# Gram matrices of the delta rule formed once for both directions, decay rows on all 128 partitions, constant buffer parts filled by GpSimd and ScalarE

## The chip, the core and the metric

One core of a Trainium2 chip (trn2). Its engines run their own instruction streams side by side: TensorE (PE; PEld is its weight load), VectorE (DVE), ScalarE (ACT), GpSimd (POOL) and SyncE (SP, which only issues DMAs here). The metric is the device time of one execution in microseconds, lower is better.

## The reference

One layer of a hybrid block over 2048 latent tokens of width 1024, with 256 context tokens ahead of them: a normalised and modulated input goes through one combined projection, then eight heads of softmax attention and four heads of a gated delta rule run in parallel on it, their outputs are normalised, concatenated and projected, and a gated feed-forward part follows. The change lies in the delta rule, which runs in both directions over the tokens:

```python
def chunk_gated_delta(q, k, v, g, beta, s0):
    """S_t = a_t (I - b_t k_t k_t^T) S_{t-1} + b_t k_t v_t^T, o_t = S_t^T q_t."""
    ...
    diff = g_cum[..., :, None] - g_cum[..., None, :]
    decay_incl = jnp.exp(jnp.where(incl, diff, -jnp.inf))
    decay_strict = jnp.where(strict, decay_incl, 0.0)
    k_beta = k * beta[..., None]
    lower = jnp.einsum("bhnid,bhnjd->bhnij", k_beta, k) * decay_strict
    t_inv = lax.linalg.triangular_solve(lower + eye, ..., left_side=True, lower=True, unit_diagonal=True)
    u = t_inv @ (v * beta[..., None])
    w = t_inv @ (k_beta * jnp.exp(g_cum)[..., None])
    ...
        intra = jnp.einsum("bhnid,bhnjd->bhnij", q, k) * decay_incl
    def step(state, xs_n):
        v_new = u_n - w_n @ state
        new_state = state * d_n + k_n^T @ v_new
        o_n = q_n @ state + a_n @ v_new

oc_f, s_ctx_f = chunk_gated_delta(qdc, kdc, vdc, gc_f, bec_f, s0)
oc_b, s_ctx_b = chunk_gated_delta(flip(qdc), flip(kdc), ..., s0)
ol_f, _ = chunk_gated_delta(qd, kd, vd, g_f, be_f, s_ctx_f)
ol_b, _ = chunk_gated_delta(flip(qd), flip(kd), ..., s_ctx_b)
o_gdn = gated_rms(ol_f + flip(ol_b), z_d, gdn_norm_g)
```

(The bodies are shortened; `step` is written here as matrix products.) The products `k k^T` and `q k^T` inside a chunk do not depend on the direction; the decays do.

## The kernel before

The program has three parts. Part one (to about 715 us of the trace) makes all projections and stores what the rest needs to DRAM: `qsc`, `ksc`, `vsc` for the attention, `gsc` (keys, queries and values of the delta rule in chunks of 128 tokens; `kd` is a piece on its way there) and `rsc` (decay rows). Part two (about 715 to 1780 us) is the attention and the delta rule together. Part three is output projection and feed-forward, to the end.

In part two `attention` takes 16 blocks of 128 queries. For each, `sm` products give a maximum (`mx`, `shift`), and then 18 pairs of key chunks follow: `sc` products (with `kh` and with `kx`, whose row 0 is a constant), the exponential `p`, its half-precision part `hp` and remainder `lp` (the latter a subtraction on GpSimd), and the products `ops` of `hp` and `lp` with the values `vst`. The number of a half and of its first key chunk stand in a name: `sc_15_1_6` is query block 15, second half, pair from chunk 6.

`delta(plan, d)` is one direction, d = 0 forward and d = 1 backward, in 18 steps of one chunk each: 2 of context, 16 latent. The two directions meet in the middle: step s of one and step 19 − s of the other work on the same latent chunk. A step loads `tT` (keys and queries, transposed), `tk` (keys and values scaled for this direction) and `rows`, 12 rows of decays, which the products `pdb`, `pdi` and `per` contract over 12 partitions to spread the decays over a 128x128 tile per head. `db` is the exponential of `pdb`; times the Gram matrix `pkk` it is the triangular matrix, which is split in `lh` and `ll` and inverted in steps (`m`, `t`, `pt`, `py`, `y`, `pa`, then `pr`, `r`, `pn`, `ti`). For latent chunks `at` is the exponential of `pdi` times the Gram matrix `pkq`. Then comes what depends on the state `s`: `pw`, `rv`, `pv`, `vn`, `pz`, the new `s`, and the output `po`, stored as `o` by the direction that comes first and added up as `fin` by the other. `y` are six buffers per direction that begin as unit matrices.

All instructions of part two are recorded (`Plan.add`; so their line in the trace is L403, where they are issued) and then issued in the order that a planner computes before the run (`Plan.order`): each engine takes, of the instructions whose inputs and ring buffers it thinks ready, the most urgent, with urgency from the track's weight. The tracks are `a` (attention, weight 1.0 by its share of work), `i0`, `i1` (what does not depend on the state, weight `IW`) and `d0`, `d1` (the rest, weight `DW`). `RINGS` says how many buffers a tile name has; the PSUM ring `g` of three banks serves all products of the delta rule, the ring `s` the `sc` products and `m` the `sm` products. On the chip each engine runs its stream in order and waits where an input is late. Loads of step 0 and the first attention loads are issued by GpSimd (`G`), all later ones by SP.

## Time and profile before

| | before |
|---|---|
| time, median of 3 runs (lowest, highest) | 3514.76 us (3511.21, 3516.85) |
| profiled execution: its time, its span in the trace | 3515.73 us, 3513.9 us |
| busy in the span: PE, DVE, ACT, POOL | 3355.6, 2298.6, 1639.6, 1410.7 us |
| mean granted clock of TensorE | 0.980 |
| part one, part two, part three (about) | 715, 1065, 1734 us |

The profile is of one execution. Busy times of PE are modelled at their ends, since matmuls are pipelined: the step from one start to the next is what an instruction advances the stream by. A row of waits is time that an engine stood idle, put down to what ended the wait.

### The profile page before, as it was taken

Reading aid. Unit: us, or ns where it says so; the run is one execution under the profiler, and the core shown is the slowest. Engines: PE = TensorE matmul, PEld = TensorE weight load, DVE = VectorE, ACT = ScalarE, POOL = GpSimd, SP = SyncE. Lnnn points to the kernel's source line nnn. Section 1 sums busy time; section 2 is a strip of 40 time slices with the busy share of each in tenths; the row PEclk is TensorE's granted clock in tenths of the full one; section 3 lists DMA queues with packets and bytes.
Section 4 is the critical chain, followed back from the end, with each engine's and each line's share of the span. In section 5 each row is a group of like instructions: output and inputs, shape, how many; then the busy total and the mean of one; then the engine's idle time right before and its main releaser. Section 6 shows DMA issues by size and latency. Waiting matters only on the chain.

```text
span 3513.9 us, 65298 instructions
## 1 busy us (share of the span) xinstructions
PE 3355.6 (95%) x26281; PEld 2715.5 (77%) x26281; DVE 2298.6 (65%) x3619; ACT 1639.6 (47%) x2556; POOL 1410.7 (40%) x1423
## 2 busy tenths in 40 slices
PE   6799999979999999999978999999999999999998
PEld 3799878857777777777756778888888888888898
DVE  5665577887777777777655567735773476447743
ACT  4443233447777676777644443323332333224331
POOL 4684455437767777777765411100110010001100
PEclk7899999989999999999989999999999999999999
DMA  6323335651111222220146643343334333433332
GB/s 227 90 66 97 120 116 149 189 153 48 60 63 55 66 63 70 66 65 29 53 145 218 218 159 96 95 130 112 120 97 124 115 116 97 125 114 120 96 108 91
DMA packets 209199, 381.30 MB, mean 109 GB/s; under 512 B 20360, under 2 KB 95720, under 8 KB 208624
## 3 DMA queue, kind: packets, MB, share of 16 engines
q1 hardware_dynamic: 207056, 371.74, 33.4%
q0 software_dynamic: 1840, 5.39, 0.6%
q8 instruction: 206, 3.38, 0.4%
q14 instruction: 97, 0.79, 0.1%
HBM read 297.73 MB, written 79.72 MB: 107 GB/s over the span
## 4 chain that ended last, share of the span: by engine, by line
PE 77%; DVE 8%; POOL 6%; DMA 4%; issue 3%; ACT 2%; SPq 0%; POOLq 0%; DVEq 0%; ACTq 0%
PE pu L520 9%; PE pu L519 9%; PE pu L521 9%; PE sc L403 6%; PE ops L403 5%; PE pdn L521 5%; PE pdn L520 5%; PE pdn L519 5%; PE po L403 3%; PE sm L403 3%; PE pa L403 1%; PE pg L520 1%; PE pg L519 1%; PE pg L521 1%; PE pkk L403 1%
## 5 line engine op out<-in xcount | busy, mean ns | idle before, releaser
L403 POOL TENSOR_TENSOR lp<-p,hp 128x1024 f16<-128x1024 f32 x288 | 616.0, 2146 | 232.8 <-DVE hp L403 88.0
L519 PE MATMUL pu<-h,ws_u 128*128 128x512 f32 x1408 | 550.5, 391 | 2.8 <-ACT h L403 2.8
L520 PE MATMUL pu<-h,ws_u 128*128 128x512 f32 x1408 | 549.0, 390 | 2.5 <-DVE h L403 2.5
L521 PE MATMUL pu<-h,ws_u 128*128 128x512 f32 x1408 | 548.5, 390 | 0.0
L403 DVE TENSOR_REDUCE mx<-sm 128x1 f32<-128x512 f32 x512 | 336.1, 681 | 74.7 <-PE sm L403 72.6
L1718 POOL COPY carry<-ue 128x2 f32<-128x2 f32 x132 | 24.8, 188 | 891.4 <-ACT ue L1716 891.4
L403 ACT ACTIVATE p<-sc 128x1024 f32<-128x1024 f32 x288 | 294.9, 1024 | 182.7 <-PE sc L403 173.3
L519 PEld LDWEIGHTS pu<-h,ws_u 128*128 128x128 f32 x1408 | 264.7, 188 | 60.1 <-ACT h L403 4.8
L520 PEld LDWEIGHTS pu<-h,ws_u 128*128 128x128 f32 x1408 | 264.6, 188 | 59.6 <-DVE h L403 4.2
L521 PE MATMUL pdn<-hid,ws_d 128*128 128x512 f32 (+2 forms) x880 | 307.4, 349 | 0.0
L520 PE MATMUL pdn<-hid,ws_d 128*128 128x512 f32 (+2 forms) x880 | 307.4, 349 | 0.0
L521 PEld LDWEIGHTS pu<-h,ws_u 128*128 128x128 f32 x1408 | 264.8, 188 | 54.9
L519 PE MATMUL pdn<-hid,ws_d 128*128 128x512 f32 (+2 forms) x880 | 306.4, 348 | 0.0
L1727 DVE SCALAR_TENSOR_TENSOR cv<-ue,cols,cv 128x512 f32<-128x512 f32 (+1 forms) x352 | 264.9, 752 | 15.8 <-DVE cv L1724 0.5
L1716 ACT COPY ue<-pu 128x512 f32<-128x512 f32 x176 | 103.2, 586 | 367.6 <-PE pu L521 367.0
L1690 DVE TENSOR_TENSOR ws_u<-raw_u,ws_u 128x1024 fp32r<-128x1024 f32 x176 | 214.5, 1219 | 19.1 <-ACT ws_u L1685 19.1
L403 PE MATMUL sc<-q,kh 128*128 128x512 f16 x576 | 218.7, 380 | 4.5 <-ACT p L403 3.9
L1724 DVE TENSOR_SCALAR cv<-ue,cols 128x512 f32<-128x512 f32 (+1 forms) x176 | 96.3, 547 | 188.3 <-ACT ue L1716 183.3
L403 PE MATMUL sc<-qx,kx 128*128 128x512 f16 x576 | 218.6, 380 | 0.0
L1715 POOL COPY ue<-carry 128x2 f32<-128x2 f32 x176 | 95.4, 543 | 291.6 <-DVE cv L1727 291.3
L1690 DVE TENSOR_TENSOR ws_d<-raw_d,ws_d 128x1024 fp32r<-128x1024 f32 (+1 forms) x96 | 109.0, 1136 | 157.8 <-ACT ws_d L1685 155.6
L403 ACT CAST hp<-p 128x1024 f16<-128x1024 f32 x192 | 200.8, 1047 | 3.3
(580 smaller groups left out, 8068.1 us busy)
## 6 DMA issues: line engine op xcount, KB each, us to landing
raw_u<-in_wu SPq DMA_DIRECT2D x176, 512.0 KB
raw_d<-in_wd SPq DMA_DIRECT2D x64, 512.0 KB
tk<-gsc SPq DMA_DIRECT2D x34, 512.0 KB
tT<-gsc SPq DMA_DIRECT2D x66, 256.0 KB
wm<-in_wm SPq DMA_DIRECT2D x64, 256.0 KB
gsc<-kd SPq DMA_DIRECT2D x64, 256.0 KB
raw_o<-in_wo SPq DMA_DIRECT2D x32, 512.0 KB
raw_d<-in_wd SPq DMA_DIRECT2D x32, 384.0 KB
```

Source lines behind the costliest of these rows:

```text
L403: fn(**{k: v.get() if isinstance(v, Lazy) else v for k, v in kw.items()})
L519: PE.matmul(out=ps, lhsT=hi_l(k), rhs=hi_r(k), start=st, stop=False)
L520: PE.matmul(out=ps, lhsT=hi_l(k), rhs=lo_r(k), start=False, stop=False)
L521: PE.matmul(out=ps, lhsT=lo_l(k), rhs=hi_r(k), start=False, stop=en)
L1690: V.tensor_tensor(out=made[u][:, 1, :n], in0=raws[u][:, :n], in1=made[u][:, 0, :n].bitcast(F32), op=ALU.subtract)
L1715: G.tensor_copy(out=ue[:, 0:2], in_=carry[:, b, :])
L1716: S.copy(out=ue[:, 2:514], in_=ps)
L1718: G.tensor_copy(out=carry[:, b, :], in_=ue[:, 512:514])
L1724: V.tensor_scalar(out=cv[:, :W], in0=ue[:, 0:W], scalar1=fw[0], scalar2=cols[:, C_FB + b:C_FB + b + 1], op0=ALU.mult, op1=ALU.add)
L1727: V.scalar_tensor_tensor(out=cv[:, :W], in0=ue[:, i:i + W], scalar=fw[i], in1=cv[:, :W], op0=ALU.mult, op1=ALU.add)
```

## The change

Three things change in part two, and two with them.

1. The direction that comes to a latent chunk first (`first`) copies each of its two Gram matrices from PSUM to a tile `gk` on ScalarE, and SP stores it to a new DRAM tensor `gmsc`. The other direction loads it (`gl`, two buffers) in place of its own products `pkk` and `pkq`.
2. The decay rows stand in two tiles of 128 partitions for the whole of part two, filled with zeros once; a step's load writes rows 0 to 11. The products contract over all 128 partitions.
3. The zeros of `rows`, `qx` and `kx` and the constant row of `kx` are filled by GpSimd ahead of its first loads, where VectorE filled `qx` and `kx` before. The `y` buffers are copied by ScalarE in place of VectorE.
4. `tk` has one buffer per direction in place of two.
5. `DW` and `IW` are 1.2 in place of 1.35, so the order of every engine in part two is another.

```diff
--- before.py
+++ after.py
@@ -36,12 +36,12 @@
 NJ = DFF // P
 EPS = 1e-6
 BIG = 1e30
-DW, IW = 1.35, 1.35
+DW, IW = 1.2, 1.2
 PSHIFT, PSLACK = 11.0, 6.5
 VTOP = 1024.0
 GTOP, ROWV, SC = 2048.0, 4096.0, 1024.0
 YB, UB = 3, 3
-RINGS = dict(s=1, m=2, o=1, g=3, p=4, hp=4, lp=4, q=2, h=4, fa=1, at=1, fb=2, tT=2, tk=2, st=2, t=2, ti=2, rw=1, fin=1)
+RINGS = dict(s=1, m=2, o=1, g=3, p=4, hp=4, lp=4, q=2, h=4, fa=1, at=1, fb=2, tT=2, tk=1, st=2, t=2, ti=2, fin=1)
 STAG = -0.03
 PATIENCE = dict(G=150.0, S=100.0)
 XB, LATER, KVW, DTB, PEC = 13, 3, 10.0, 5, 4.0
@@ -436,6 +436,7 @@
     ksc = dram.tile([NCK, P, KV, P], F16, name="ksc")
     vsc = dram.tile([NCK, P, 128], F32, name="vsc")
     zsc = dram.tile([NTT, P, 512], F32, name="zsc")
+    gmsc = dram.tile([NCK, 2, P, 512], F32, name="gmsc")
     osc = dram.tile([NTT, P, 512], F32, name="osc")
     osm = dram.tile([NTT, P, 512], F32, name="osm")
     oat = dram.tile([NTT, P, 512], F32, name="oat")
@@ -1070,11 +1071,11 @@
     pc = ExitStack()
     c2 = pc.enter_context(tc.tile_pool(name="c2", bufs=1, side="right", reuse_waits="tile"))
     kb = c2.tile([P, B_ER], BF16, name="kb")
-    er = c2.tile([12, P], BF16, name="er")
+    er = c2.tile([P, P], BF16, name="er")
     i16 = c2.tile([P, HG * P], F16, name="i16")
     lv16 = c2.tile([P, K_END - K_LV], F16, name="lv16")
     G.dma_start(out=kb, in_=kb_d[:, 0:B_ER])
-    G.dma_start(out=er, in_=kb_d[0:12, B_ER:B_END])
+    G.dma_start(out=er, in_=kb_d[:, B_ER:B_END])
     G.dma_start(out=lv16, in_=k32_d[:, K_LV:K_END])
     n16 = c2.tile([P, P], F16, name="n16")
     V.tensor_scalar(out=n16, in0=ident, scalar1=-1.0, scalar2=None, op0=ALU.mult)
@@ -1091,6 +1092,14 @@
     gf = p2.enter_context(tc.tile_pool(name="gf", bufs=5, reuse_waits="tile"))
     ap = p2.enter_context(tc.tile_pool(name="ap", bufs=4, side="right", reuse_waits="tile"))
     psa = p2.enter_context(tc.tile_pool(name="psa", bufs=1, space=PSUM, reuse_waits="tile"))
+    rows_t = [gs.tile([P, HG, 3, P], BF16, name=f"rows{d}", bufs=1) for d in range(2)]
+    qx_t = [ak.tile([P, HA, P], F16, name=f"qx{i}", bufs=1) for i in range(2)]
+    kx_t = ak.tile([P, NCK, KV, P], F16, name="kx", bufs=1)
+    for t in rows_t:
+        G.memset(t, 0.0)
+    for t in qx_t + [kx_t]:
+        G.memset(t[0:64], 0.0)
+    G.memset(kx_t[0:1], ROWV)
     plan = Plan(tc, psa)
     plan.patience, plan.rate, plan.fixed = PATIENCE, 2.34, (150, 55, 200, 170, 25)
 
@@ -1110,10 +1119,7 @@
             return plan.tile(psa, [P, 2, 512], F32, "s", n_, RINGS["s"])
 
 
-        qxs = [plan.tile(ak, [P, HA, P], F16, f"qx{i}", f"qx{i}", 1) for i in range(2)]
-        for t in qxs:
-            V.tensor_scalar(out=t[0:64], in0=ones[0:64, :].unsqueeze(1).broadcast_to([64, HA, P]), scalar1=0.0, scalar2=None,
-                            op0=ALU.mult)
+        qxs = [plan.wrap(t, [P, HA, P], F16) for t in qx_t]
 
         def load_q(qb):
             qt = plan.tile(aq, [P, HA, P], F16, "q", f"q_{qb}", RINGS["q"])
@@ -1126,16 +1132,12 @@
 
         q_now = load_q(0)
         kh = plan.tile(ak, [P, NCK, KV, P], F16, "kh", "kh", 1)
-        kx = plan.tile(ak, [P, NCK, KV, P], F16, "kx", "kx", 1)
+        kx = plan.wrap(kx_t, [P, NCK, KV, P], F16)
         for a in range(0, NCK, 6):
             src = ksc[a:a + 6].rearrange("c p f t -> p c f t")
             G.dma_start(out=kh[0:64, a:a + 6], in_=src[0:64])
             G.dma_start(out=kh[64:128, a:a + 6], in_=src[0:64])
         loaded.append(len(plan.ops) - 1)
-        for g in range(KV):
-            V.tensor_scalar(out=kx[0:64, :, g, :], in0=ones[0:64, :].unsqueeze(1).broadcast_to([64, NCK, P]), scalar1=0.0,
-                            scalar2=None, op0=ALU.mult)
-            V.tensor_scalar(out=kx[0:1, :, g, :], in0=ones[0:1, :].unsqueeze(1).broadcast_to([1, NCK, P]), scalar1=ROWV, scalar2=None, op0=ALU.mult)
         for a in range(0, NCK, 6):
             G.dma_start(out=kx[64:128, a:a + 6], in_=ksc[a:a + 6].rearrange("c p f t -> p c f t")[64:128])
 
@@ -1267,6 +1269,7 @@
     lv0 = lv16[:, 0:P].unsqueeze(1).broadcast_to([P, HG, P])
     bid = kb[:, B_ID:B_ID + P]
     o_l = [plan.wrap(osc[i], [P, 512], F32) for i in range(NTT)]
+    gm_l = [[plan.wrap(gmsc[i, j], [P, 512], F32) for j in range(2)] for i in range(NCK)]
 
     FT = {n: (t, RINGS[t]) for t, ns in (("fa", "db qe"), ("at", "at"), ("ti", "ti"), ("fb", "rv vn o")) for n in ns.split()}
 
@@ -1283,11 +1286,14 @@
         ys = [None]
         for l in range(1, 7):
             y = plan.tile(gh, [P, 512], F16, f"y{d}{l}", f"y{d}{l}", 1)
-            V.tensor_copy(out=y, in_=i16)
+            S.copy(out=y, in_=i16)
             ys.append(y)
         lvm = [None] + [lv16[:, P + 64 * (6 * d + l):P + 64 * (6 * d + l + 1)].bitcast(U16) for l in range(6)]
         ms = kb[:, (B_MSB if d else B_MSF):][:, :P].unsqueeze(1).broadcast_to([P, HG, P])
         mi = kb[:, (B_MIB if d else B_MIF):][:, :P].unsqueeze(1).broadcast_to([P, HG, P])
+
+
+        rws = plan.wrap(rows_t[d], [P, HG, 3, P], BF16)
 
         for step in range(NCK):
             ck = chunk_of(d, step)
@@ -1296,6 +1302,7 @@
             lat = ck >= NCC
             last = step == NCK - 1
             first = step < NCK + NCC - 1 - step if lat else step == 0
+            held = []
             q = SY if step else G
             plan.gate = None if step else loaded[0]
             tT = plan.tile(gin, [P, 2, 512], F32, f"tT{d}", f"tT_{nm}", RINGS["tT"])
@@ -1304,9 +1311,12 @@
                 SY.dma_start(out=tT[:, 1, :], in_=gsc[ck, :, 5, :])
             tk = plan.tile(gin, [P, 2, 512], F32, f"tk{d}", f"tk_{nm}", RINGS["tk"])
             q.dma_start(out=tk, in_=gsc[ck, :, 1 + 2 * d:3 + 2 * d, :])
-            rws = plan.tile(gs, [12, HG, 3, P], BF16, f"rows{d}", f"rows_{nm}", RINGS["rw"])
-            q.dma_start(out=rws, in_=rsc[d, ck].rearrange("h r s t -> r h (s t)"))
+            q.dma_start(out=rws[0:12], in_=rsc[d, ck].rearrange("h r s t -> r h (s t)"))
             plan.gate = None
+            if lat and not first:
+                for i in range(2):
+                    held.append(plan.tile(gin, [P, 512], F32, f"gl{d}", f"gl_{nm}_{i}", 2))
+                    SY.dma_start(out=held[i], in_=gm_l[ck][i])
 
             def bank(n_):
                 return plan.tile(psa, [P, 512], F32, "g", f"{n_}_{nm}", RINGS["g"])
@@ -1351,10 +1361,18 @@
             db = f32t("db")
             S.activation(out=db, in_=pd_, func=AF.Exp)
             def gram(i):
+
+                if held:
+                    return held[i]
                 pk = bank("pkq" if i else "pkk")
                 with plan.group():
                     for h in range(HG):
                         PE.matmul(out=pk[:, hs[h]], lhsT=tT[:, 0, hs[h]], rhs=tT[:, i, hs[h]], start=True, stop=True)
+                if not lat:
+                    return pk
+                gk = plan.tile(gin, [P, 512], F32, f"gk{d}", f"gk_{nm}_{i}", 1)
+                S.copy(out=gk, in_=pk)
+                SY.dma_start(out=gm_l[ck][i], in_=gk)
                 return pk
 
             V.scalar_tensor_tensor(out=db, in0=gram(0), scalar=-1.0, in1=db, op0=ALU.mult, op1=ALU.mult)
```

Three places show what stands where. TensorE at the start of step 12 of direction 0, a chunk that the other direction has had at its step 7: first before, where the four `rows` products are followed by the four products of the Gram matrix.

```order
L403 LDWEIGHTS kb_8056
L403 MATMUL pdb_0_12_19207<-kb_8056 128x512
L403 LDWEIGHTS rows_0_12_19146
L403 MATMUL pdb_0_12_19207<-rows_0_12_19146 128x128
...
L403 MATMUL pkk_0_12_19215<-tT_0_12_18593 128x128 x4
L403 MATMUL pv_0_11_19222<-rv_0_11_18610,ti_0_11_19203 128x128 x4
```

The same place now.

```order
L403 LDWEIGHTS kb_8057
L403 MATMUL pdb_0_12_19945<-kb_8057 128x512
L403 LDWEIGHTS rows0_8094
L403 MATMUL pdb_0_12_19945<-rows0_8094 128x128
...
L403 LDWEIGHTS t_1_11_19846
L403 MATMUL pa1_1_11_19954<-y11_8125,t_1_11_19846 128x64
```

The Gram product is gone; the weights come from the tile that stands for the whole part, and the stream goes on with the other direction's inversion.

GpSimd at the seam from part one to part two, with its DMA issues (`u` is the last piece of part one): before,

```order
L1055 MEMSET u_11_3_7999 128x1
L403 DMA q_0_8095<-qsc_61 128x1024
L403 DMA kh_8105<-ksc_62 64x6x256 x5
L403 DMA qx0_8129<-qsc_61 64x1024
L403 DMA kh_8105<-ksc_62 64x6x256
L403 DMA tT_0_0_8148<-gsc_60 128x512
L403 DMA rows_0_0_8150<-rsc_71 12x4x384
L403 DMA tT_1_0_8155<-gsc_60 128x512
L403 DMA rows_1_0_8158<-rsc_71 12x4x384
L403 DMA tk_0_0_8160<-gsc_60 128x1024
L403 DMA tk_1_0_8163<-gsc_60 128x1024
L403 DMA kx_8146<-ksc_62 64x6x256 x3
```

and now

```order
L1099 MEMSET rows0_8094 128x1536
L1099 MEMSET rows1_8095 128x1536
L1101 MEMSET qx0_8096 64x1024
L1101 MEMSET qx1_8097 64x1024
L1101 MEMSET kx_8098 64x4608
L403 DMA q_0_8107<-qsc_61 128x1024
L403 DMA qx0_8096<-qsc_61 64x1024
L403 DMA kh_8129<-ksc_62 64x6x256 x6
...
L403 DMA kx_8098<-ksc_62 64x6x256
L1102 MEMSET kx_8098 1x4608
L403 DMA kx_8098<-ksc_62 64x6x256 x2
L403 DMA tk_0_0_8186<-gsc_60 128x1024
```

Five fills stand ahead of the first load `q`, and the fill of the constant row stands between two loads of `kx`; the loads of `tk` have moved behind those of `kx`.

TensorE at the last product of the delta rule, `po` of step 17 of direction 1 (four of eight rows are left out): before,

```order
L403 LDWEIGHTS kx_8146
L403 MATMUL sc_15_1_6_27647<-qx1_8132,kx_8146 128x512
L403 MATMUL po_1_17_27654<-s_1_16_26590,tT_1_17_26592 128x128
L403 MATMUL po_1_17_27654<-vn_1_17_27610,at_1_17_27548 128x128
...
L403 LDWEIGHTS hp_15_1_4_27637
L403 MATMUL ops_15_1_27593<-vst_8624,hp_15_1_4_27637 128x65
```

and now

```order
L403 LDWEIGHTS q_15_26042
L403 MATMUL sm_15_1_0_2_27116<-kh_8129,q_15_26042 128x512
L403 MATMUL po_1_17_27118<-s_1_16_25534,tT_1_17_25478 128x128
L403 MATMUL po_1_17_27118<-vn_1_17_27038,at_1_17_26893 128x128
...
L403 LDWEIGHTS lp_14_1_14_27095
L403 MATMUL ops_14_1_26753<-vst_8551,lp_14_1_14_27095 128x65
```

Before, 20 `sc` products (five pairs of query block 15) stand behind it; now the `sc` products of all 18 pairs of block 15 do, 72 of them, with part of the block's `sm` products.

## Rows read from the trace of the kernel before

**Rows 1.** Busy time of the engines by stretch; columns: the stretch, its length, busy us of PE, PEld, DVE, ACT and POOL (with instructions), granted TensorE clock, busy share of the 16 DMA engines (1 is all, packets of two transfers can overlap), GB/s.

```profile
715.00:740.00 25.00, 10.46 (x46) 6.48 (x45) 17.55 (x33) 8.45 (x20) 5.37 (x7) 0.63 1.06 319
740.00:900.00 160.00, 152.04 (x2143) 114.09 (x2142) 134.98 (x243) 109.53 (x152) 99.19 (x54) 0.97 0.16 50
900.00:1740.00 840.00, 829.54 (x11797) 624.02 (x11796) 636.25 (x1131) 600.92 (x774) 611.14 (x322) 1.00 0.20 61
1758.00:1780.20 22.20, 12.67 (x181) 8.15 (x178) 7.75 (x8) 11.13 (x15) 19.88 (x14) 0.84 0.20 49
```

**Rows 2.** Waits of PE from 757 to 1758 us, the largest entry: us in total, times, longest.

```profile
PE pt L403 <- DVE t L403: 5.1, 8, 1.4
```

**Rows 3.** Gram products. First the timeline of PE from 763 us (start, us, then the instruction, xcount), then PE's groups by shape from 720 to 1785 us (xcount | busy us, mean ns | idle before).

```profile
763.21 1.16 PE L403 MATMUL pkk<-tT 128*128 128x128 f32 x8
764.21 0.38 PE L403 MATMUL sm<-kh,q 128*128 128x512 f16 x1
764.42 0.38 PE L403 MATMUL sc<-q,kh 128*128 128x512 f16 x1
...
L403 PE MATMUL pkk<-tT 128*128 128x128 f32 x288 | 41.6, 289 | 2.6 <-DVE s L403 1.4 <-ACT db L403 1.2
...
L403 PE MATMUL pkq<-tT 128*128 128x128 f32 x256 | 35.3, 281 | 0.0
```

**Rows 4.** Timeline of PE around the decay rows, 1748.5 to 1752 us.

```profile
1749.20 0.38 PE L403 MATMUL pdi<-kb 128*128 128x512 bf16 x1
1749.51 0.39 PE L403 MATMUL pdi<-rows 12*128 12x128 bf16 x4
1749.83 1.16 PE L403 MATMUL pkq<-tT 128*128 128x128 f32 x8
...
1751.25 0.40 PE L403 MATMUL pn<-r,t 128*128 128x128 f16 x4
1751.48 0.41 PE L403 MATMUL ops<-vst,lp 128*128 128x65 f16 x8
```

**Rows 5.** Weight loads of the decay rows, by shape, 720 to 1785 us (xcount | busy us, mean ns | idle before, what ended it).

```profile
L403 PEld LDWEIGHTS <-rows 12*128 12x128 bf16 x272 | 15.1, 93 | 23.8 <-issue 23.0 <-DMA vraw<-vsc 0.8
...
L403 PEld LDWEIGHTS <-er 12*128 12x128 bf16 x128 | 7.1, 92 | 9.6 <-issue 9.1
```

**Rows 6.** The seam: timeline of PE, of DVE and of POOL (idle before it and what ended that in brackets), the fill that is nearest to the new ones (min/median/max ns), and the issue row of `kh` from 703 to 740 us (queue, xcount, KB each, median us from issue to landing).

```profile
710.69 0.60 PE L958 MATMUL pt<-k,y 128*128 128x128 f32 x4
...
720.14 1.12 PE L958 MATMUL pt<-k,y 128*128 128x128 f32 x4 [4.28 <-ACT y L1022]
729.33 1.11 PE L958 MATMUL pt<-k,y 128*128 128x128 f32 x4 [8.07 <-ACT y L1022]
730.24 1.06 PE L403 MATMUL sm<-kh,q 128*128 128x512 f16 x2
...
719.55 2.01 DVE L403 TENSOR_SCALAR qx<-k 64x1024 f16<-64x1024 f32 x2
721.49 2.60 DVE L403 TENSOR_SCALAR kx<-k 64x2304 f16<-64x2304 f32 x2
...
706.16 0.54 POOL L403 DMA_DIRECT2D q<-qsc  x1 [0.36 <-issue]
706.70 3.30 POOL L403 DMA_DIRECT2D kh<-ksc  x5
...
L897 POOL MEMSET rt<- x2: 3934/3934/3935, 306.2 to 326.7; 72x4608 bf16 x2
...
kh<-ksc POOLq DMA_DIRECT2D x6, 192.0 KB, 5.6
```

**Rows 7.** The chain of work that ended last, pieces from 717 to 738 us (start, us, what).

```profile
718.07 16.69 DMA gsc<-kd
...
737.31 0.61 ACT db L403
```

**Rows 8.** VectorE from 740 to 1758 us: an operation with one input in PSUM, and two with both in SBUF; xcount: duration ns min/median/max, first and last start.

```profile
L403 DVE SCALAR_TENSOR_TENSOR db<-pkk,db x35: 659/681/692, 739.5 to 1724.5; 128x512 f32<-128x512 f32 x35
...
L403 DVE TENSOR_TENSOR m<-lh,lv x36: 411/1024/2160, 740.1 to 1727.1; 128x512 f16<-128x512 f16 x36
...
L403 DVE TENSOR_TENSOR t<-i,m x36: 407/776/1750, 741.3 to 1728.0; 128x512 f16<-128x512 f16 x36
```

**Rows 9.** Timeline of all engines at 1796 us (part three), POOL and DVE.

```profile
1796.29 2.34 POOL L403 TENSOR_TENSOR ws_o<-raw_o,ws_o 128x1024 fp32r<-128x1024 f32 x1
1796.35 2.82 DVE L403 SCALAR_TENSOR_TENSOR oraw<-oraw,oss,rows 128x512 f32<-128x512 f32 x1 [1.06 <-POOL oss L403]
```

**Rows 10.** ScalarE's copy of a 128x512 product out of PSUM, by shape, 740 to 1740 us (xcount | busy us, mean ns | idle before).

```profile
L403 ACT COPY vn<-pv 128x512 f32<-128x512 f32 x35 | 20.4, 583 | 13.0 <-PE pv L403 12.5
```

**Rows 11.** One `tk` load: timeline of PE, SP and DVE from 1520 to 1530 us, and the busy tenths of the DMA engines in 40 slices of 1521.9 to 1529.9 us.

```profile
1521.09 1.06 PE L403 MATMUL pz<-vn,tk 128*128 128x128 f32 x8
...
1522.18 0.32 SPq L403 DMA_DIRECT2D tk<-gsc  x1
...
1529.06 1.13 DVE L403 SCALAR_TENSOR_TENSOR rv<-pw,kbe,tk 128x128 f32<-128x128 f32 x4
...
DMA  0000009913599976100000000000000000957899
```

**Rows 12.** Timeline of POOL at the end of the attention.

```profile
1773.02 6.73 POOL L403 TENSOR_TENSOR lp<-p,hp 128x1024 f16<-128x1024 f32 x3
```

## Prediction, made before the changed kernel was run

> **What bounds the kernel now.** I read the windows first, to find the stage that the change touches. From 740 to 1740 us, where both directions of the delta rule run beside the attention, TensorE (PE) is busy 829.54 of 840 us and 152.04 of 160, at a granted clock of 1.00 (the upper of its two levels, 2.4 GHz) and 0.97; VectorE, ScalarE and GpSimd are near three quarters, and the DMA engines at a fifth [rows 1]. The waits of PE come next: over 1,001 us the largest entry is 5.1 us, behind the delta chain's `t` [rows 2]. So PE's own instruction stream is the limit there, and work taken off it is time, as long as no other engine comes up to it. Two stretches are of another kind: the seam before the stage, 715 to 740, with PE busy 10.46 of 25 us and the DMA engines full, and its end, 1758 to 1780, with five attention pairs left, GpSimd busy 19.88 of 22.2 us and PE 12.67 [rows 1].
>
> **The change, part by part.**
>
> *Grams.* Each latent chunk's two Gram matrices are now formed by the direction that comes first; 32 of 68 groups leave PE (eight records each: 36 groups of `pkk`, 32 of `pkq`). From the start of one `pkk` to the next instruction is 764.21 − 763.21 = 1.00 us; the engine's busy time gives 41.6/36 = 1.16 and 35.3/32 = 1.10, modelled ends included [rows 3]. A 512-column half-precision product beside it advances 0.21, so nothing else hides in the 1.00. That piece enters from a 12-row group, which the next term counts, so I take 0.93: 32 × 0.93 = **−30 us** (bounds −28 and −32).
>
> *Decay rows on 128 partitions.* The columns streamed do not change, only the height of the array in use. Going into the 12-row group, a 512-column product advances 1749.51 − 1749.20 = 0.31 instead of 0.21; coming out, four products advance 1749.83 − 1749.51 = 0.32, where four of the same width at full height (`pn`) advance 1751.48 − 1751.25 = 0.23 [rows 4]. So a group of short rows costs 0.10 + 0.09 = 0.19 us beyond its work. The weight loads say the same from the other side: 272 loads of `rows` stand idle 23.8 us and 128 of `er` 9.6, nearly all put down to issue [rows 5]. There are (272 + 128)/4 = 100 groups, hence 100 × 0.19 = **−19 us**; if the gap is the group's own and not its height's, 0.
>
> *The seam.* VectorE loses the fills of `qx` (2.01 us) and `kx` (2.60 for the zeros alone) and twelve copies, which stood between the last pieces of the projections: PE waited 4.28 and 8.07 us for `y` there, and its first attention product came only at 730.24. GpSimd gets five fills ahead of `q`. The nearest row, a fill of 72x4608 bf16, takes 3.93 us [rows 6]; by columns that makes 1.31 twice for `rows`, 0.87 twice for `qx`, 3.93 for `kx`, 8.3 us, and another 3.93 between two loads of `kx`. By the order the first fill waits for the last projection tile but one, whose products end where `pt` begins, at 710.69; so `q` is issued near 719 instead of 706.16, and the last `kh`, 4 to 5 us behind it, near 724. The `kh` loads took 5.6 us to land [rows 6], so `sm` starts near 730 as before. What ends the seam is not that but the store of `kd`, 16.69 us in the chain, with the last `kd` and a table load between its end and `db` at 737.31 [rows 7]; the store ran while the DMA engines were full [rows 1]. With VectorE's queue 5 us shorter and the loads of `kx`, `tk` and `vraw` later than the stores, the last `kd` is done some 5 us sooner. I take **−4 us** (bounds −8, and +13 if the loads behind the fills decide).
>
> *The held Grams on VectorE.* The 32 `db` and `at` operations of the second direction now read two SBUF tiles; with PSUM they take 681 ns with hardly any spread [rows 8]. The two-SBUF-input product `m` has 411 least, 1024 in the middle and 2160 at most [rows 8]. One pair of rows shows how: GpSimd starts `ws_o` at 1796.29 for 2.34 us, VectorE's `oraw` with two SBUF inputs starts 0.06 later and lasts 2.82, 0.5 past GpSimd's end [rows 9]. The Trainium skill, page "SBUF — State Buffer", section "Who interferes with whom", states it as a rule: a VectorE instruction with two SBUF inputs contends with a GpSimd instruction that reads SBUF, and the later issuer is blocked for the whole of the other. Here the trace agrees, and the rule speaks against this part of the change.
> On average I add what `m` has over its least, 0.6 us, plus 0.1: 32 × 0.7 = 22 us more on VectorE, in its second 500 us. What reaches PE is far less: `m` and `t` together already lose about 36 × (0.6 + 0.4) = 36 us so, and PE waits 5.1 us for `t` [rows 2, 8]. That ratio gives 22 × 5/36 = 3; I take **+4** (bounds 0 and 68, the latter 32 × (2.82 − 0.68), rows 8 and 9 at their worst).
>
> *Copies on ScalarE.* 32 copies of a Gram at 583 ns, the time of `vn` from PSUM [rows 10], are 19 us in the first half, on an engine that is 72% busy; twelve `y` copies are some 7 us at the seam, where it is busy 8.45 of 25 [rows 1]. A Gram's PSUM bank is held a copy longer. **+3** (0 to +10).
>
> *Stores and loads.* 64 transfers of 256 KB are 17 MB in a stage whose DMA share is 0.20 [rows 1]: no cost in bandwidth. Two new waits: SP's queue holds each store until its copy is done, with the prefetches behind it, which are issued well ahead of their use; and step 10 of one direction needs step 9 of the other through DRAM. **+1** (0 to +4).
>
> *One `tk` buffer.* The load can now be issued only after `pz`. In the trace the issue stands at 1522.18, just behind `pz` (1521.09, 1.06 long), and the next reader `rv` at 1529.06; its transfer shows as busy slices of 0.2 us from the seventh to the eighteenth after 1521.9, so it is in by 1525.5 [rows 11]: 3.3 us from the issue, of 6.9. In the new order `pw` stands 1 to 5 us of PE work behind `pz` in the first ten steps, so some ten loads are late by a fraction. **+3** (0 to +10).
>
> *The order.* The lower weights let the attention take turns earlier; before, the last delta product stood ahead of the last five pairs, now ahead of eighteen. There PE has no delta work to fill the wait for `lp`, and GpSimd needs 6.73/3 = 2.24 us a pair [rows 12] and the same 19.88 − 11.2 = 8.7 us of output work: 18 × 2.24 + 8.7 = 49 us. PE's part is at most 18 × 12.67/5 = 46 and, at the upper clock instead of 0.84, some 38. So PE waits 3 to 11 us there, against 22.2 − 12.67 = 9.5 now [rows 1]. **+1** (−6 to +8).
>
> *Sum:* −30 − 19 − 4 + 4 + 3 + 1 + 3 + 1 = −41. The profiled execution took 3515.7 us, 1 us above the median of the runs; 3515.7 − 41 = **3475 us**, 1.2% less. Nothing after 1785 us is touched.
>
> **Rivals.**
> - *The held Grams lock VectorE against GpSimd (slower).* The place is steps 10 to 17 of both directions, the price up to 2.14 us each. Without that term the sum is −45; it turns the sign when 45/32 = 1.4 us of each reaches PE, and at 2.14 the time is 3515.7 − 45 + 68 = 3539. For it: GpSimd is busy 73% of the stage and one `lp` lasts 2.1 us. Against it: the 7-to-1 cushion above, and an average delay near 0.7. 6 in 100. The rule of the Trainium skill's page "SBUF — State Buffer" named above would give this case if each operation met a fresh `lp`.
> - *The bare tail drags.* If eighteen pairs run like the last five (22.2/5 = 4.4 us each), the tail is 80 us instead of 49: 3475 + 31 = 3506, still faster. For it: nothing but attention is there to cover a wait. Against it: two thirds of the pairs lie ahead of the output work that slowed those five. 10 in 100.
> - *The rows change does nothing,* because the 0.19 us belong to loading new weights in small groups: 3494. Against it, `pn`, also four small products, has no such gap. 8 in 100.
> - *The seam waits for GpSimd's fills:* +13 instead of −4, 3492. 10 in 100.
> - *The work leaves PE, but the stage does not shorten,* since the reordered chains of the two directions now meet their latencies: PE has stalled little, yet a step's chain of some 25 dependent links fills its slot. Giving back all 49 us means 3515 to 3525, no change or a little slower. 7 in 100.
>
> **How the numbers follow.** The forecast has 59 in 100 and its own range, with about half of the terms at their nearer bounds at once, 3462 to 3488. The whole range takes in the rows, seam and tail cases and leaves out the two bad ones: 3456 to 3506. About 0.2%, 7 us, is what a measurement of this kernel can tell from no change. Faster by more than that: the forecast and the three mild cases, 87 in 100. Within it: half of the last case and a few near the turning point of the first, 5. Slower: 8.
>
> **What would show it.** Right: `pkk` and `pkq` with 544 − 32 × 8 = 288 records together; the `rows` loads with their issue idle near nothing; PE's busy time of the stage down by about 45 to 50 us and its waits much as before; first `db` earlier than 737.3; `db` and `at` in a second, longer form from the held tiles. Wrong: PE waits for `db`, `at` or `t` of tens of us in the second half (the lock); waits for `lp` above 20 us at the end (the tail); a wait of PE on `tk` or `gl` loads. The prediction fails most easily where I had no row: the latencies of the new order.

## The result, and the profile after

The changed kernel takes 3489.72 us (median of 6 runs, 3483.83 to 3492.77) against 3517.35 us of the kernel before beside it: a ratio of 0.992 [0.9905, 0.9934], 28 us less. A second set of runs gave 0.9927 [0.9915, 0.9939]. The forecast was 41 us less, 3475 us, within 3456 to 3506.

Parts one and three, which the change hardly touches, differ by several us from one execution to the next (part three lasted from 1731 to 1743 us in the profiled executions), so I compare part two inside each trace: from the start of the last projection product `pg` to that of the first `pto` product of part three. That is 1065.2 us before, and 1037.1 us after (1040.3 in the second profile): 25 to 28 us, the whole difference.

The windows of the kernel before, cut at the first `pdb`, half-way to the last `po`, at the last `po` and at the first `pto` (stretch, length, busy us of PE first):

```profile
715.00:732.20 17.20, 4.32 (x17) 2.47 (x16) 14.87 (x28) 4.32 (x12) 4.74 (x6) 0.59 1.05 299
732.20:1245.00 512.80, 498.44 (x7036) 376.76 (x7035) 396.77 (x715) 362.27 (x490) 344.11 (x184) 0.99 0.20 64
1245.00:1757.50 512.50, 505.45 (x7175) 377.70 (x7172) 384.06 (x676) 365.82 (x461) 381.05 (x199) 1.00 0.18 57
1757.50:1780.20 22.70, 13.17 (x191) 8.64 (x190) 8.25 (x8) 11.13 (x15) 19.99 (x16) 0.84 0.19 48
```

and of the changed kernel, cut at the same places of the program:

```profile
711.60:726.40 14.80, 4.99 (x21) 2.87 (x20) 8.66 (x13) 12.43 (x29) 14.21 (x15) 0.77 1.01 274
726.40:1211.00 484.60, 467.64 (x6787) 361.23 (x6786) 375.90 (x684) 364.01 (x492) 340.24 (x185) 0.99 0.25 80
1211.00:1694.80 483.80, 465.36 (x6792) 353.16 (x6790) 408.68 (x677) 354.50 (x464) 368.91 (x192) 0.99 0.28 87
1694.80:1748.70 53.90, 39.55 (x561) 24.14 (x559) 26.06 (x32) 33.49 (x37) 47.27 (x28) 0.96 0.11 26
```

PE's busy time in part two fell from 1021.4 to 977.5 us, so 44 us of work left it; its idle time (length less busy) rose from 43.8 to 59.6. The second profile of the changed kernel (e5 below) has 980.2 and 60.1, 41 us less work. By stretch, the idle time went from 12.9 to 9.8 us at the seam, 14.4 to 17.0 in the first half, 7.1 to **18.4** in the second half, 9.5 to **14.4** at the end. VectorE does more in the second half than it did in the longer one before: 408.68 of 483.8 us against 384.06 of 512.5.

The work that left, in PE's groups by shape and the weight loads (answers [rows 3, 5]; xcount | busy, mean ns | idle before):

```profile
L403 PE MATMUL pkk<-tT 128*128 128x128 f32 x160 | 21.9, 280 | 0.0
...
L403 PE MATMUL pkq<-tT 128*128 128x128 f32 x128 | 17.3, 278 | 0.0
...
L403 PEld LDWEIGHTS <-rows 128*128 128x128 bf16 x272 | 20.8, 98 | 10.3 <-issue 0.6 <-DMA rows<-rsc 0.4
...
L403 PEld LDWEIGHTS <-er 128*128 128x128 bf16 x128 | 9.2, 98 | 1.4 <-issue 0.5
```

288 Gram records are left of 544. The idle put down to issue ahead of the `rows` and `er` loads went from 32 us to 1, all idle ahead of them from 33.4 to 11.7. The first `db` exponential, a sign that the prediction named, comes at 727.0 us in place of 737.3. A piece of PE's timeline shows both prices (answers [rows 3, 4]):

```profile
728.19 0.38 PE L403 MATMUL pdb<-kb 128*128 128x512 bf16 x1
728.40 0.39 PE L403 MATMUL pdb<-rows 128*128 128x128 bf16 x4
728.63 1.11 PE L403 MATMUL pkk<-tT 128*128 128x128 f32 x8
729.57 0.78 PE L403 MATMUL sm<-kh,q 128*128 128x512 f16 x2
```

The 512-column product ahead of the rows now advances 0.21 us in place of 0.31, the four rows products 0.23 in place of 0.32, and a Gram takes 0.94.

The products with a loaded Gram on VectorE (answers [rows 8]; min/median/max ns). From 1240 to 1690 us their means are 1.30 us for `db` and 1.72 for `at`:

```profile
L403 DVE SCALAR_TENSOR_TENSOR db<-gl,db x16: 679/1236/2283, 1233.9 to 1636.7; 128x512 f32<-128x512 f32 x16
...
L403 DVE TENSOR_TENSOR at<-gl,at x16: 676/1912/2652, 1279.1 to 1681.3; 128x512 f32<-128x512 f32 x16
```

One place shows how such a product comes to hold up TensorE (timelines of POOL, DVE and PE):

```profile
1329.13 2.14 POOL L403 TENSOR_TENSOR lp<-p,hp 128x1024 f16<-128x1024 f32 x1 [0.28 <-POOL lp L403]
1329.53 2.28 DVE L403 SCALAR_TENSOR_TENSOR db<-gl,db 128x512 f32<-128x512 f32 x1 [0.18 <-ACT db L403]
...
1334.02 2.27 POOL L403 TENSOR_TENSOR lp<-p,hp 128x1024 f16<-128x1024 f32 x1
1334.57 2.01 DVE L403 TENSOR_TENSOR t<-i,m 128x512 f16<-128x512 f16 x1
1336.63 0.40 PE L403 MATMUL pt<-i,t 128*128 128x128 f16 x4 [1.51 <-DVE t L403]
```

The held `db` starts 0.4 us behind an `lp` of GpSimd and ends 0.54 us past its end; `t`, which also reads two SBUF tiles, does the same 5 us later. VectorE has no pause between the two, and PE waits 1.51 us for `t`. Of the 17.3 us of waits that PE's list has in the second half, 16.2 end with a VectorE instruction. I followed VectorE's work without a pause back from each of these, up to 12 us: what the held products there take beyond 0.68 us covers 12.3 of the 16.2 us, counting no wait for more than its length. That is a bound from above, since other work stands in the same stretches.

### The profile page after: what moved, and what is told of

It is laid out like the page before. It is cut to its first block, busy times and chain, and to the rows that moved or that the text cites. A ratio compares the mean times of both kernels' runs of the same rounds, so it can differ in the third digit from the quotient of the medians.

```text
span 3482.1 us, 64968 instructions
## 1 busy us (share of the span) xinstructions
PE 3309.7 (95%) x26025; PEld 2692.3 (77%) x26025; DVE 2312.2 (66%) x3601; ACT 1661.9 (48%) x2600; POOL 1432.9 (41%) x1429
## 4 chain that ended last, share of the span: by engine, by line
PE 73%; DVE 10%; POOL 6%; DMA 4%; issue 3%; ACT 3%; SPq 0%; POOLq 0%; DVEq 0%; ACTq 0%
PE pu L521 9%; PE pu L522 9%; PE pu L520 9%; PE sc L403 6%; PE ops L403 5%; PE pdn L522 5%; PE pdn L521 5%; PE pdn L520 5%; PE po L403 3%; PE sm L403 2%; PE pa L403 1%; DVE mx L403 1%; PE pg L522 1%; PE pg L521 1%; PE pg L520 1%
## 5 line engine op out<-in xcount | busy, mean ns | idle before, releaser
L403 POOL TENSOR_TENSOR lp<-p,hp 128x1024 f16<-128x1024 f32 x288 | 623.3, 2172 | 212.2 <-DVE hp L403 66.9
```

What stands on the lines that cost most here:

```text
L403: fn(**{k: v.get() if isinstance(v, Lazy) else v for k, v in kw.items()})
```

## The experiments

Every kernel below is the changed one but for the lines shown, except e3 and e6, which start from the kernel before. Part two is measured as above; idle is PE's, for the seam, the two halves and the end.

| kernel | ratio to before, 95% interval | part two, us | idle: seam, first, second half, end |
|---|---|---|---|
| before | 1 | 1065.2 | 12.9, 14.4, 7.1, 9.5 |
| changed | 0.9920 [0.9905, 0.9934] | 1037.1 | 9.8, 17.0, 18.4, 14.4 |
| e5 the same again | 0.9927 [0.9915, 0.9939] | 1040.3 | 10.3, 17.2, 18.5, 14.2 |
| e1 exponentials in PSUM | 0.9904 [0.9892, 0.9917] | 1030.3 | 10.4, 16.5, 12.0, 12.6 |
| e2 six `lp` on VectorE | 0.9937 [0.9925, 0.9949] | 1037.3 | 10.8, 16.5, 18.3, 12.7 |
| e3 rows alone | 0.9974 [0.9966, 0.9983] | 1054.3 | 12.6, 16.9, 8.0, 12.6 |
| e4 weights 1.35 | 0.9936 [0.9923, 0.9949] | 1040.5 | 10.2, 15.9, 17.8, 14.0 |
| e6 Grams alone | 0.9965 [0.9952, 0.9977] | 1050.3 | 13.1, 11.9, 13.7, 11.6 |
| e7 weights 0.85 | 0.9919 [0.9905, 0.9932] | 1035.7 | 11.1, 16.5, 19.2, 9.2 |
| e8 fills and copies back | 0.9917 [0.9903, 0.9930] | 1037.4 | 12.6, 18.0, 13.1, 13.3 |
| e9 `y` copies on VectorE | 0.9933 [0.9920, 0.9945] | 1037.3 | 10.5, 16.2, 18.4, 13.2 |
| e10 e1 and e9 | 0.9894 [0.9879, 0.9909] | 1029.7 | 10.5, 16.2, 12.1, 12.9 |
| e11 e10, weights 0.85 | 0.9878 [0.9864, 0.9892] | 1023.3 | 12.1, 15.6, 7.6, 10.3 |
| e12 e10, output work on VectorE | 0.9898 [0.9884, 0.9912] | 1028.9 | 10.0, 16.3, 12.1, 12.9 |

**e1: the ports.** Where a Gram is loaded, the exponentials stay in PSUM:

```diff
-            S.activation(out=db, in_=pd_, func=AF.Exp)
+            S.activation(out=pd_ if lat and not first else db, in_=pd_, func=AF.Exp)
-            V.scalar_tensor_tensor(out=db, in0=gram(0), scalar=-1.0, in1=db, ...)
+            V.scalar_tensor_tensor(out=db, in0=gram(0), scalar=-1.0, in1=pd_ if held else db, ...)
```

(and the same for `at` with `pd2`; the lines are shortened).

> The changed kernel, with one difference: where a Gram matrix is loaded, the exponentials db and at are left in their PSUM bank, so that VectorE's product reads one SBUF tile and one PSUM bank. No instruction is added or removed; the bank is held until the product is done. Theory A (the two-SBUF products wait for GpSimd, and that reaches PE): the held db and at fall from means of 1.30 and 1.72 us to about 0.68, VectorE gets back 26 us, PE's waits between 1240 and 1680 us fall from 16 us towards the 4 us of the kernel before, and the time falls by 8 to 15 us against the changed kernel (ratio to before about 0.988 to 0.990 in place of 0.992). Theory B (the waits come from the new order and the meeting of the two directions, not from the ports): db and at get shorter all the same, but PE's waits stay at 12 us or more and the time within 4 us.

The products lost their spread (min/median/max ns), and the second half of the mixed stretch its idle time in part:

```profile
L403 DVE SCALAR_TENSOR_TENSOR db<-gl,pdb x16: 667/678/689, 1237.5 to 1629.1; 128x512 f32<-128x512 f32 x16
...
L403 DVE TENSOR_TENSOR at<-gl,pdi x16: 670/677/689, 1283.3 to 1673.6; 128x512 f32<-128x512 f32 x16
...
1204.00:1681.10 477.10, 465.10 (x6848) 354.01 (x6845) 390.77 (x688) 357.51 (x467) 361.90 (x192) 1.00 0.28 88
```

Idle there is 12.0 us in place of 18.4, part two 7 to 10 us shorter, the ratio 0.002 lower. By the time that is theory A, at or just under the low end of its 8 to 15 us; the waits went about half of the way that it gave them. One doubt remains: the longer hold of the bank also changes the planner's order (TensorE's stream is another from about the middle on, with 21 pairs behind the last `po`), and e8, with another order and the old products, has 13.1 us there too. So how much of the 6.4 us is the ports and how much the order was not separated. Over all kernels the sign of the edit holds: with the old products part two lasts 1035.7 to 1040.5 us in four orders (e4, e7 and e8 have others), with the new ones 1023.3 to 1030.3 in two.

**e2: the end, by moving `lp`.** Three `lp` of each half of query block 15 by VectorE:

```diff
-                G.tensor_tensor(out=lp, in0=pr, in1=hp, op=ALU.subtract)
+                (V if qb == NTT - 1 and c0 // 2 in (2, 5, 7) else G).tensor_tensor(out=lp, in0=pr, in1=hp, op=ALU.subtract)
```

> The changed kernel, with the subtraction lp of six of the last eighteen attention pairs moved from GpSimd to VectorE. Theory A (the stretch without delta work, 1680 to 1749 us, is bound by GpSimd's lp at 2.1 us a pair): PE's wait for lp there falls from 9.6 us to under 4, the stretch from 68.5 to about 58 us, the time falls by 6 to 12 us. Theory B (the stretch is bound by PE's own work and the chain of one pair): 0 to 3 us.

GpSimd's busy time at the end fell from 47.3 to 35.4 us, the stretch from 53.9 to 52.2 only, and part two is as long as in the changed kernel. Theory B.

**e3: rows alone.** On the kernel before:

```diff
-    er = c2.tile([12, P], BF16, name="er")
+    er = c2.tile([P, P], BF16, name="er")
...
+    rows_t = [gs.tile([P, HG, 3, P], BF16, name=f"rows{d}", bufs=1) for d in range(2)]
+    for t in rows_t:
+        G.memset(t, 0.0)
...
-            rws = plan.tile(gs, [12, HG, 3, P], BF16, f"rows{d}", f"rows_{nm}", RINGS["rw"])
-            q.dma_start(out=rws, in_=rsc[d, ck]...)
+            q.dma_start(out=rws[0:12], in_=rsc[d, ck]...)
```

> The kernel before, with only the decay rows on 128 partitions (two standing tiles, zeros by GpSimd, er with 128 partitions). Theory A (a short row group costs 0.19 us beyond its work): the idle time ahead of the rows and er loads goes to about nothing, and the time falls by 15 to 20 us (ratio about 0.995). Theory B (the gap belongs to small groups as such): the idle stays and the time is within 3 us of before.

The idle ahead of the loads went to 4.2 us (issue), and PE's busy time fell by 17.2 us, as worked out; but the gain is 9 us by the runs and 10.9 in part two. 14 pairs now stand behind the last `po`, and idle rose by 2.5 us in the first half (one `pdb`, the other direction's first, waits 2.9 us for `kd` in place of 0.5) and 3.1 at the end. Both theories missed the time: the price is right and not all of it arrives.

**e4 and e7: the weights.**

```diff
-DW, IW = 1.2, 1.2
+DW, IW = 1.35, 1.35    (e4)
+DW, IW = 0.85, 0.85    (e7)
```

> The changed kernel with the weights DW and IW back at 1.35; all else as in the change. The last delta product then stands ahead of about 28 attention pairs in place of 18. Theory A (pairs without delta work beside them cost PE about 0.5 to 0.7 us of waiting for lp each): 5 to 8 us slower than the changed kernel, ratio to before about 0.994. Theory B (earlier delta work gives the chains more room, which is worth more than the tail): as fast or faster than the changed kernel, with fewer waits of PE before the tail.

> The changed kernel with the weights DW and IW at 0.85; all else as in the change. The last delta product then stands ahead of five attention pairs, as before the change, in place of 18. Theory A (a stretch of attention alone costs PE more waiting, the longer it is: 13 us with five pairs, 20.5 with 18): the wait at the end falls by about 7 us, and the time by 4 to 8 us against the changed kernel. Theory B (delta work that is issued later meets its own latencies instead): PE's waits for t, y and s grow by as much, and the time stays within 3 us or rises.

At 1.35 the time is the same within the intervals (part two 0 to 3 us longer, 27 pairs behind the last `po`, the idle time not higher), which decides for neither theory. At 0.85 the end shrinks from 53.9 to 22.8 us and its idle from 14.4 to 9.2, but the second half keeps 19.2, and the time of the runs stays within 3 us of e5: theory B. Alone, the weights decide little between 0.85 and 1.35.

**e5: the yardstick.**

> The changed kernel itself once more, as a yardstick for the runs beside it on this chip. Both theories: ratio to before 0.990 to 0.994, with PE's last delta product near 1,695 us and about 54 us from it to part three.

The ratio is as expected. The last `po` stands at 1703.0, 8 us late: 5 of these come from part one, and the last stretch is again 53.9 us.

**e6: Grams alone.** The kernel before with `gmsc` and, of the change's diff, the lines with `held` and `gk`, and `tk=1` for the room:

```diff
+            if lat and not first:
+                for i in range(2):
+                    held.append(plan.tile(gin, [P, 512], F32, f"gl{d}", f"gl_{nm}_{i}", 2))
+                    SY.dma_start(out=held[i], in_=gm_l[ck][i])
...
+                S.copy(out=gk, in_=pk)
+                SY.dma_start(out=gm_l[ck][i], in_=gk)
```

> The kernel before with only the Gram matrices shared (copy, store, load, one tk buffer for the room); decay rows on 12 partitions, fills and weights as before. PE has 32 groups fewer, some 29 us. Theory A (the two-SBUF products of the second direction and the longer stretch without delta work give more than half of it back): 8 to 15 us faster than before, ratio 0.996 to 0.998, PE's stalls in the second half of the mixed stretch up by 10 us or more. Theory B (the Gram work is gained in full and the loss sits in the other parts): 24 to 29 us faster, ratio about 0.992.

12 us faster by the runs, 14.9 in part two: theory A by the time, though the idle time of the second half rose by nearly 7 us and not by its 10 or more. In the first half, where nearly all copies and stores stand, it fell from 14.4 to 11.9. Rows alone and Grams alone together make 25.8 us of part two, the change 25 to 28: within the 3 us between two profiles of one kernel they add, and the seam and the weights bring nothing on top.

**e8 and e9: the seam.** e8 has both edits below, with VectorE's fills where they stood before; e9 has only the second.

```diff
-    for t in qx_t + [kx_t]:
-        G.memset(t[0:64], 0.0)
-    G.memset(kx_t[0:1], ROWV)
...
-            S.copy(out=y, in_=i16)
+            V.tensor_copy(out=y, in_=i16)
```

> The changed kernel with the seam undone: VectorE fills qx and kx and copies the y buffers again, GpSimd only the two rows tiles. Theory A (the fills stood between the last pieces of the projections on VectorE): the last pt product of part one moves from about 722 back to about 729 us, the first sc from 745 to about 756, and the time rises by 4 to 9 us. Theory B (the loads behind the fills in GpSimd's queue decide, so the change gained nothing here): the first sc comes no later than in the changed kernel, and the time is the same or less.

> The changed kernel with one part undone: the twelve y buffers are copied by VectorE again (the fills stay on GpSimd); the order on TensorE is the same. In the changed kernel's chain of waits nine y copies of 0.53 us each stand on ScalarE between the last projection products and the last pieces of kd. Theory A (these copies took the place of VectorE's fills as what the seam waits for): the first pdb comes 4 to 6 us earlier after the last projection product (10 to 12 us in place of 14.8 to 16.2), and the time falls by 2 to 5 us against the changed kernel. Theory B (the loads behind the fills on GpSimd's queue come next at once): pdb comes no more than 1.5 us earlier, no change of the time.

Neither changes the time. From the last `pg` to the first `pdb` it is 17.2 us before, 14.8 and 16.2 after, 16.9 in e8, 16.4 in e9. In e8 the first `sc` does come 3 to 7 us later than in the changed kernel, counted from the last `pg`, as its theory A says, but the time does not rise; e9 is theory B. The chain of waits shows what stands behind the copies; of the changed kernel:

```profile
713.51 4.77 ACT y L403 x9
...
719.93 1.04 ACT y L1023 x2
...
721.02 1.98 PE pt L959 x8
```

and of e9:

```profile
710.97 3.88 POOL kx L1101
...
715.94 3.35 POOL kh L403 x5
719.28 7.15 DMA kh<-ksc
...
726.57 0.60 PE sm L403
```

With VectorE free, ScalarE's `y` copies stand in front of the last `kd` pieces; with these moved, GpSimd's fills, the `kh` issues behind them and their landing are next, 16 us in a row that end at the same place.

**e10 to e12: together.** e10 joins e1 and e9; e11 adds weights of 0.85; e12 adds to e10:

```diff
+            E = V if lt in (4, 5) else G
-            G.tensor_scalar(out=ss[:, 0:1], ...)
-            G.tensor_scalar(out=ss[:, 1:], ...)
-            G.tensor_tensor(out=og, in0=og, in1=oz, op=ALU.mult)
+            E.tensor_scalar(out=ss[:, 0:1], ...)
+            E.tensor_scalar(out=ss[:, 1:], ...)
+            E.tensor_tensor(out=og, in0=og, in1=oz, op=ALU.mult)
```

> The changed kernel with the held exponentials left in PSUM (as in e1) and the y copies on VectorE (as in e9). Theory A (the two losses lie at different places and add): 10 to 13 us faster than the changed kernel, ratio to before 0.988 to 0.990, from the last projection product to part three 1,025 to 1,029 us in place of 1,037 to 1,040. Theory B (the earlier start only lengthens the stretch of attention alone at the end): as e1, 1,030 us, ratio 0.9904.

> As e10, with the weights DW and IW at 0.85, so that eight attention pairs stand behind the last delta product in place of 21. Theory A (the stretch of attention alone costs PE 0.4 to 0.5 us a pair beyond the first five): 4 to 6 us less waiting there and 2 to 5 us less time than e10. Theory B (delta work issued later meets its own latencies): the same time as e10 or more, with new waits of PE ahead of py, pz or pa.

> As e10, with six small operations of part three (two scalings each and the product with the gate, for the first two row tiles) on VectorE in place of GpSimd, where they stand between the lp subtractions of the last attention block. Theory A (these operations hold up lp, and so PE, at the end): PE's stall in the stretch behind the last delta product falls by 3 to 5 us and so does the time. Theory B (that stretch is set by the chain of one pair, with a single sc buffer): within 2 us of e10.

e10 has the time of e1 in part two, 1029.7 us against 1030.3 (theory B; its ratio of 0.9894, whose interval holds both forecasts, would also fit theory A), and e12 that of e10 (theory B): neither the copies nor the output work on GpSimd is what the time waits for. e9 and e10 differ only by e1's edit and the order that comes with it, and ran beside the same runs of the kernel before: 3492.47 and 3478.52 us, with intervals that do not touch, and part two 7.6 us shorter. e11 is the fastest kernel, 3472.62 us, 6 us below e10 (their intervals overlap; in part two it is 6.4) and 15 to 17 below the changed kernel. Its windows:

```profile
711.50:735.60 24.10, 11.99 (x31) 3.69 (x30) 19.48 (x36) 6.64 (x17) 19.15 (x20) 0.57 0.96 280
735.60:1220.00 484.40, 468.83 (x6773) 346.55 (x6772) 382.95 (x659) 372.56 (x465) 375.29 (x192) 0.99 0.18 58
1220.00:1705.10 485.10, 477.55 (x7082) 377.06 (x7080) 387.29 (x715) 363.74 (x507) 341.84 (x188) 1.00 0.33 104
1705.10:1734.80 29.70, 19.38 (x275) 12.21 (x275) 10.55 (x11) 16.40 (x20) 27.75 (x19) 0.89 0.15 37
```

The second half is back at 7.6 us of idle and the end at 10.3. Theory A is right in the time and not in its reason: the end gives 2.6 us, not 4 to 6, and the second half 4.5. With the two-SBUF products in place the same weights gave e7 less, 1 to 5 us of part two, and nothing in the second half.

## Why the prediction was right in sign and range, and a third of its gain did not come

The forecast was 49 us of work off PE and 8 us of new costs. The work came off; the costs were about 22 us: 16 us more idle time and some 6 us by which PE's other products became slower. The 3490 us measured lie inside the whole range but 2 us above the forecast's own, 3462 to 3488, and near the rivals of 3492 and 3494, neither of which took place. That a range widened for those rivals holds the result is in part luck.

- *Grams, −30 and rows, −19.* The prices were right: 0.94 us a Gram, 0.10 and 0.09 us at the two ends of a row group, now gone. PE's busy time fell by 41 to 44 us. Taken from each start to the next, idle left out, the Gram products and those around the decay rows fell from 120.2 to 70.9 us (72.2 in e5), which is the forecast; all other products of part two rose from 901.3 to 906.8 (907.9). A stall shorter than the modelled end of a matmul counts as busy, so some of the new waiting may hide there. This was not shown.
- *Held Grams, +4.* The step that failed in size. VectorE's part was nearly right (22 us forecast; means of 1.3 and 1.7 us make 26). What I took from rows was the share that reaches PE, 5 in 36 from `m` and `t` [rows 2, 8]. e1 puts it at 6 to 10 us of 26, a quarter or more, the order that comes with e1's edit included. The cushion was measured where VectorE was 76% busy; in the second half it is 84%. That this is why it gave way is argued: no run varies VectorE's load alone. What is late on VectorE delays all that stands behind it in its stream, so PE's waits grew not at `db` but elsewhere. Before, the largest from 1245 to 1757 us:

```profile
PE pt L403 <- DVE t L403: 2.4, 4, 0.8
PE sc L403 <- ACT p L403: 2.1, 6, 0.5
PE pa L403 <- DVE y L403: 0.8, 2, 0.5
```

and after, from 1211 to 1695 us (us in total, times, longest), all four behind VectorE:

```profile
PE pt L403 <- DVE t L403: 6.4, 7, 1.9
PE sm L403 <- DVE mx L403: 3.1, 8, 1.1
PE pa L403 <- DVE y L403: 2.9, 4, 1.0
PE po L403 <- DVE s L403: 2.0, 1, 2.0
```
- *The order, +1.* The end was worked out as 49 us with 3 to 11 of waiting; it lasted 53.9 with 14.4, so +5. I had GpSimd's sum as its limit. e2 and e12 take 12 and 4 us off GpSimd there and the stretch hardly moves, so it is not the sum. Most of the waiting is for single `lp` all the same (changed kernel, 1694.8 to 1748.7 us):

```profile
PE ops L403 <- POOL lp L403: 9.6, 12, 3.6
...
PE sc L403 <- ACT p L403: 1.8, 3, 0.8
```

  In e2 the waits for `lp` of both engines are still 7.1 us. Whether the chain of one pair sets the length, as theory B of e2 has it, stays open.
- *The seam, −4.* From the last `pg` to the first `pdb` it was −1 to −2.4, to the first `db` −5 to −7; the idle time of the seam and the first half together stayed as it was (27.3 us before, 26.8 after). I counted what VectorE lost and hid the copies on ScalarE under idle time [rows 1], where they were in the chain. The fills on GpSimd, the rival of +13, come one step behind, as e9 shows.
- *ScalarE +3, stores and loads +1, one `tk` buffer +3.* In the changed kernel no engine's list of waits names `gl`, and `tk` stands there once, 3.4 us of VectorE in two waits. e6 has all three parts, and its idle time in the first half is 2.5 us lower than before; the change's is 2.6 higher, as with rows alone. So no cost of these parts is to be seen there, where 7 us were put. (The transfer in [rows 11] ends a slice earlier than I read it, at 1525.3 us; the term does not hang on that.)
- *What stays open:* of the 11.4 us that the second half's idle time rose, e1 removes 6.4. The other 5 went with the weights of 0.85 (e11) and not with those of before the change (e4, 17.8 us). What is left in e1 stands nearly all behind VectorE too, 10.0 of 10.9 us, after work in which `m` and `t`, with two SBUF inputs in every kernel, take longer than their least; whether that is the cause was not tested.
- *The rivals.* The lock exists and is dear, but far from 1.4 us on PE for each product: 0.2 to 0.3. The rows did gain. The bare tail took 5 us more than forecast, not 31. The stage did shorten, by a little over half of what left PE; "waits much as before", a sign of being right, did not hold.

With e1's edit and the delta work issued later (e11), part two is 41.9 us shorter than before, as much as the forecast. That does not prove its terms: e11 still has 45.5 us of idle time, about as much as before, and the 7 us for ScalarE, stores and `tk` were too many where others were too few.

## What to carry to other kernels

When a product is shared by storing it, see from where its reader now takes it: an operand that moves from PSUM to SBUF can make a VectorE instruction wait for GpSimd, and leaving the other operand in PSUM took that wait away here, with no instruction more. A cushion measured at one load of an engine need not hold at a higher one. Work moved out of a queue at a seam must be followed to its new queue, up to the chain of waits there.

## What the runs showed of the hardware

A wait can cost PE more than its length. After the wait of 3.56 us at the end of the attention, the granted clock is 0.50, the lower of its two levels (1.2 of 2.4 GHz), for about 2.5 us (changed kernel, timeline of PE and two windows, with the clock ahead of the last two numbers):

```profile
1710.87 0.62 PE L403 MATMUL ops<-vst,lp 128*128 128x65 f16 x8 [3.56 <-POOL lp L403]
1711.30 1.07 PE L403 MATMUL ops<-vst,hp 128*128 128x65 f16 x16
1712.18 0.62 PE L403 MATMUL sc<-q,kh 128*128 128x512 f16 x1
1712.59 0.63 PE L403 MATMUL sc<-qx,kx 128*128 128x512 f16 x1
...
1715.10 0.38 PE L403 MATMUL sc<-q,kh 128*128 128x512 f16 x1
1715.32 0.38 PE L403 MATMUL sc<-qx,kx 128*128 128x512 f16 x1
...
1710.90:1713.40 2.50, 2.50 (x27) 1.72 (x28) 1.67 (x3) 0.00 (x0) 2.50 (x2) 0.50 0.00 0
1714.00:1717.00 3.00, 2.12 (x30) 1.27 (x29) 2.49 (x1) 2.57 (x3) 3.00 (x3) 1.00 0.02 5
```

The same product advances 0.41 us there and 0.22 three us later. The two longest waits of the second half, 1.97 and 1.93 us, are followed by a clock of 0.50 for 3.4 us each, at 1488.4 and 1543.0 us. GpSimd's long fills went by their columns, as reckoned: 3.94 us for 64x4608 and 3.93 for one row of 4608; the two of `rows` and the two of `qx` took 2.97 and 1.84 us where 2.62 and 1.74 were reckoned. A part of the program that only e12 touched (part three) varied by 11 us between executions, more than most of the effects studied here; the cuts inside one trace told them apart where the medians could not.
